# One order of loops, one set of addresses and one pool size in a two-layer hybrid block

## The chip, the core and the metric

The kernel runs on 1 core of one Trainium2 chip. The metric is the device time of one execution in microseconds (us). Five queues of instructions run beside each other: PE (TensorE, matrix products), ACT (ScalarE), DVE (VectorE), POOL (GpSimd) and SP (SyncE, which here issues transfers). PEld is the loading of the stationary operand of a product on PE.

## The reference, cut to what matters

Two layers run one after the other on `x`, 512 rows of 1024 floats. A layer normalises the rows, multiplies them by `w_in` (1024 x 9312), feeds the columns of the product to three mixers (an mLSTM, a gated linear attention and a sparse attention that picks 128 keys for each query), and multiplies what they give by `w_out` (2048 x 1024).

```python
p = split_columns(rmsnorm(x, norm_g) @ w_in)
...
y = jnp.concatenate([y_ml, y_gla, y_dsa], axis=-1) @ w_out
return x + y
```

All is float32. The kernel forms each product with `w_in` and `w_out` from two halves of each operand, `hi` (rounded to a one-pass format) and `lo` (what is left), as hi·hi + hi·lo + lo·hi: three one-pass matmuls (`mm3`) in place of one exact one.

## The kernel before, in words

**Weights.** `w_in` and `w_out` are packed in the order of use into 178 pieces of 128 x 1024 floats, 89 for a layer. A piece is loaded into a place called `raw` by a DMA from SP's queue, ACT makes `hi` of it, DVE makes `lo`, and `raw` is then free. All three come from one ring of 11 places (`W_BUFS`, tag "w"), with at most 3 (`RAWS`) places taken by pieces not yet split. `make_room` issues loads, `prepare` makes one `hi` or one `lo`, `give_back` frees a piece's two places when its last product has been issued, and so lets the next load be issued. A unit (a "wide" product of 512 columns, or a part of `w_out`) has 4 pieces and 96 matmuls.

**Products.** `wide` (output tile `pn`) takes a 128 x 128 slice of `xhi` or `xlo` as the stationary operand and 512 columns of a weight piece as the moving one. `proj_t` (`pt`) takes a slice of weights as the stationary operand and 512 columns (384 for the index queries) of `xhi` or `xlo` as the moving one. `w_out_part` (`pw`) takes a slice of `yhi` or `ylo` as the stationary operand and 512 columns of a weight piece as the moving one. The products inside the mLSTM (`psS` from `ml_q`, `ml_k`; `pom` from `swh`, `swl`, `vah`, `val`) and the index scores (`pss`) are one-pass too; transposes (`psx`, `psq`, `psy`, ...) and the rest are exact float32 products.

**Order in w_out.** Four blocks of 128 rows (`sb` 0 to 3) and two halves of 512 columns give 8 chunks of 12 matmuls, each a sum over two pieces. Chunks go in pairs of blocks: half 0 of blocks 0 and 1, half 1 of blocks 0 and 1, then the same for blocks 2 and 3. A piece is given back when block 3 has used it. `wide` already runs its last two blocks side by side: both blocks use piece 0, then both piece 1, and so on.

**Planner.** The order of all instructions is written out by the Python program as it runs. `Meter` gives every instruction a cost, `Clock` keeps a planned time for each engine, and `Background` emits steps of the mixers (with their transposes and small products) between products, at each `tick`, when their planned due time is not later than PE's planned time. A one-pass product of 512 columns costs max(512, 256)/2210 + 0.002 = 0.2337 us in this plan, a transpose 0.109.

**Addresses.** In each partition the program's tiles lie one pool after another, each rounded up to 32 bytes. In the program of this kernel `xhi` starts at byte 36064 and `xlo` at 52448, both 32 past a multiple of 64. The places for weights start at 75072 and the 4 KB tiles of tag "t4" (`yhi`, `ylo`, `ml_q`, `ml_k`, `ik`, ...) at 120128: both are multiples of 64, and so is every place behind them, as each is 4096 bytes long. `vah` starts 32 past a multiple, `val` on one, the eight `swh` and `swl` tiles 32 past.

Of the kernel before, what the change touches and what calls it, by code (L numbers as in the profile page):

```python
# [10 lines left out]
F32 = mybir.dt.float32  # L11
# [148 lines left out]
def free_size(ap):  # L160
    return math.prod(ap.shape[1:])


class Meter:
# [16 lines left out]
    def cost(self, op, args, kw):  # L181
        out = args[0]
        if op == "dma_start":
            return None
        if self.name == "pe":
            if op == "transpose":
                return 0.109
            n, one_pass = free_size(out), kw["rhs"].dtype == F32R
            if one_pass:
                return max(n, 256) / 2210 + 0.002  # L190
            if out.shape[0] == 64:
                return max(n / 950, 0.08)
            return max(4 * n, 256) / 2400 + 0.004
        n = free_size(args[1]) if op == "max" else free_size(out)
        pointers = sum(hasattr(v, "ap") and free_size(v) == 1 for v in (*args[2:], *kw.values()))
        accum = kw.get("accum_out") is not None
        if self.name == "act":
            switch = self.clock.ln != (args[2] == AF.Ln)
            self.clock.ln = args[2] == AF.Ln
            return 0.155 + n / 1138 + 0.09 * pointers + 0.12 * accum + 1.3 * switch  # L200
        if self.name == "dve":
            return 0.15 + n / 945 + 0.06 * min(pointers, 1) + 0.02 * accum
        if kw.get("op") == OP.pow:
            return 0.45 + 0.15 * n
        return 0.1 + n / (510 if op == "tensor_tensor" else 600) + 0.1 * (op == "tensor_tensor")


class Clock:
# [4 lines left out]
    def __init__(self):  # L213
        self.at = dict(pe=0.0, act=0.0, dve=0.0, pool=0.0, sync=0.0)
        self.now = 0.0
        self.ln = True
        self.written, self.touched = {}, {}
        self.rings = {}

    def begin(self):  # L220
        self.now = self.at["pe"]
# [112 lines left out]
def hybrid_kernel(ctx, tc, a, out, dbg=None):  # L334
# [12 lines left out]
            nc.gpsimd.dma_start(dbg[name], ap)  # L347

    ctx.enter_context(tc.manual_schedule())
    N_T4, N_T2 = 11, 19  # L350
    W_BUFS, RAWS, LOAD = 11, 3, 4.5
    const = ctx.enter_context(tc.tile_pool(name="const", bufs=1))
    par = ctx.enter_context(tc.tile_pool(name="par", bufs=2))
    wp = ctx.enter_context(tc.tile_pool(name="wp", bufs=2))
# [6 lines left out]
    def pp(name):  # L361
        t = psp.tile([128, 512], F32, tag="pp", name=name)
        clock.ring("pp", t, 3)
        return t
# [35 lines left out]
    nc.vector.memset(head, 0.0)  # L400
    for odd, r in enumerate(HALVES):
        nc.vector.memset(head[r, odd:odd + 1], 1.0)
    xhi = const.tile([128, KT, S], F32R, name="xhi")
    xlo = const.tile([128, KT, S], F32R, name="xlo")
    qzs = [const.tile([128, 2, 64 * NB], F32, name=f"qz{i}") for i in range(2)]
    for t in qzs:
        for odd, r in enumerate(HALVES):
            nc.gpsimd.memset(t[r, 1 - odd], 0.0)
    lev = const.tile([128, len(LEVELS), 32], U8, name="lev")


    def rstd_of(ss, n, dim, rs, scale=1.0):
# [75 lines left out]
    def need(p):  # L488
        while p.parts is None:
            if not half_done:  # L490
                clock.at["pe"] = max(clock.at["pe"], to_split[0].loaded)
            prepare()
        return p.parts
# [10 lines left out]
    def give_back():  # L504
        p = held.pop(0)
        wanted.remove(p)
        state["used"] -= 2
        make_room()
# [7 lines left out]
    def mm3(ps, lh, ll, rh, rl, first, last):  # L516
        nc.tensor.matmul(ps, lhsT=lh, rhs=rh, start=first, stop=False)
        nc.tensor.matmul(ps, lhsT=lh, rhs=rl, start=False, stop=False)
        nc.tensor.matmul(ps, lhsT=ll, rhs=rh, start=False, stop=last)
# [148 lines left out]
    for layer in range(DEPTH):  # L668
# [53 lines left out]
        def w_out_part(q, yt, tasks, after=None):  # L722
            pieces = take("out", 512 * q)

            def chunk(sb, half):
                bg.drain(tasks[sb])
                s = slice(128 * sb, 128 * sb + 128)
                c = slice(512 * half, 512 * half + 512)
                ps = pp("pw")
                for k in range(4):  # L730
                    wh, wl = need(pieces[2 * half + k // 2])
                    yhi, ylo = (t[k // 2][:, k % 2, s] for t in yt)
                    mm3(ps, yhi, ylo, wh[k % 2], wl[k % 2], k == 0, k == 3)
                    if k % 2:
                        if sb == NB - 1:
                            give_back()
                        if k == 1:
                            tick()
                nc.vector.tensor_tensor(xr[:, sb, c], ps, xr[:, sb, c], op=OP.add)
                if after == "store":  # L740
                    nc.sync.dma_start(out[0, s, c], xr[:, sb, c])
                elif after == "norm" and half:
                    norms.append(norm_task(layer + 1, sb))
                tick()

            for pr in range(2):
                for half in range(2):
                    for sb in (2 * pr, 2 * pr + 1):
                        chunk(sb, half)

# [64 lines left out]
        def scores(i, iqs, ikh, ikl):  # L817
            n = 128 * (i + 1)
            iw = L["iw"]
            acc = wk.tile([128, n], F32, tag=f"acc{i}", name=f"acc{i}", bufs=1)  # L820

            def add(h, rel):
                sc = iw[:, 8 * i + h:8 * i + h + 1]
                if h == 0:
                    nc.vector.tensor_scalar(acc, rel, sc, None, op0=OP.mult)
                else:
                    nc.vector.scalar_tensor_tensor(acc, rel, sc, acc, op0=OP.mult, op1=OP.add)

            pend = []
            for pair in range(4):  # L830
                pss = [pa("pss") for _ in HALVES]
                qs = [iqs[pair // 2][pair % 2][:, odd, 128 * (i - 1):128 * i] for odd in range(2)]
                for q, ps in zip(qs, pss):
                    nc.tensor.matmul(ps[:, 0:n], lhsT=q, rhs=ikh[:, 0:n], start=True, stop=False)
                for r, q, ps in zip(HALVES, qs, pss):
                    nc.tensor.matmul(ps[:, 0:n], lhsT=q[r], rhs=ikl[r, 0:n], start=False, stop=True)
                for p in pend:
                    add(*p)
                pend = []
                for odd, ps in enumerate(pss):  # L840
                    rel = t2("relu", n)
                    nc.scalar.activation(rel, ps[:, 0:n], AF.Relu, scale=0.125)
                    pend.append((2 * pair + odd, rel))
                yield
            for p in pend:
                add(*p)
            D_(f"score{i}", acc)
            nc.gpsimd.memset(acc[0:64, n - 64:n], NEG_INADM)
            accs[i] = acc
            yield  # L850
# [430 lines left out]
        def ml_unit(h):  # L1281
            got, dst, convs, va, t_va = {}, {}, [], [], []
            states[h] = got
            for which, name in enumerate(("ml_q", "ml_k")):
                def part(b, ps):
                    if which not in dst:
                        if not which:
                            bg.drain(t_gates, *(t_scores if h else ()))
                            products_done(h)
                        dst[which] = [blocks(t4(name, dtype=F32R), 2) for _ in range(2)]  # L1290
                    convs.append(bg.start(conv(dst[which], ps, b, 8 * which + 2 * h + b), "conv"))
                chunks_t(take("in", OFF[name] + 256 * h), part)
            done["ml", h] = [bg.add(ml_values(h, got, hn_m), "mlv")]
            bg.add(ml_products(h, dst[0], dst[1], convs, got, done["ml", h - 1] if h else []), "ml")
            so = blocks(t4("so"), NB)

            def part(sb, ps):
                d = so[:, sb, :]
                nc.scalar.activation(d, ps[:, 0:256], AF.Tanh, scale=0.5)
                nc.gpsimd.tensor_scalar(d, d, 0.5, 0.5, op0=OP.mult, op1=OP.add)  # L1300
                if not va:
                    if h:
                        bg.drain(*done["ml", h - 1])
                    va.extend(wk.tile([128, NB, 258], F32R, tag=n, name=n, bufs=1) for n in ("vah", "val"))
                    for t, v in zip(va, (1.0, 0.0)):
                        nc.gpsimd.memset(t[:, :, 256:258].bitcast(F32), v)
                t_va.append(bg.start(split_task([(ps[:, 256:512], va[0][:, sb, 0:256], va[1][:, sb, 0:256])]), "split"))
            wide(take("wide", OFF["ml_o"] + 256 * h), part)
            got["values"] = (so, va, t_va)
# [42 lines left out]
```

## Time and profile before

| | us |
|---|---|
| median of 3 runs | 1228.73 (1228.69 to 1230.84) |
| the profiled execution | 1227.63 |
| its span, first to last instruction | 1225.9 |
| PE busy | 1198.3 (98% of the span) |
| DVE busy | 835.1 (68%) |
| ACT busy | 600.6 (49%) |

The shares of busy time are means over the span; a matmul's busy time is longer than its share of a dense run, since matmuls overlap, so what a matmul costs is read from the distance between starts. Idle time of an engine is put down to what released it.

### The profile page before, as it was taken

How to read it: one execution, taken by the hardware profiler on the slowest of the kernel's cores; microseconds unless marked ns; L12 is line 12 of the kernel's file. 1: busy time of each engine (PE TensorE's matmuls, PEld its weight loads, DVE VectorE, ACT ScalarE, POOL GpSimd, SP SyncE). 2: the span in 40 equal slices, each digit the busy share in tenths (PEclk: the TensorE clock that was granted, in tenths of full speed). 3: DMA queues.
4: the chain of work that ended last, by engine and by line, in shares of the span. 5: the costliest groups of instructions: out<-in, count | busy, mean ns of one | idle time of the engine just before them, and what ended most of it. 6: DMA issues, size and time to landing. Idle time of an engine off the chain costs nothing. (4 is left out here: it accounts for less than half of the span.)

```text
span 1225.9 us, 16513 instructions
## 1 busy us (share of the span) xinstructions
PE 1198.3 (98%) x6004; PEld 970.6 (79%) x6004; DVE 835.1 (68%) x1650; ACT 600.6 (49%) x1334; POOL 171.0 (14%) x309
## 2 busy tenths in 40 slices
PE   6999899999999999999999999999999999999998
PEld 4877687888888887788879777888788888778887
DVE  5477797876777765355555888879867867544644
ACT  6565446554344354652366654474443443555421
POOL 2001221321000010210010023031210000122000
PEclk8999999999999999999999999999999999999999
DMA  5333122212332234132124222222222223233221
GB/s 195 108 98 104 44 92 72 86 61 55 105 108 69 70 119 129 53 112 86 69 70 128 63 86 79 80 73 86 71 70 86 79 85 104 70 112 112 69 82 73
DMA packets 35152, 107.70 MB, mean 88 GB/s; under 512 B 5028, under 2 KB 8388, under 8 KB 35072
## 3 DMA queue, kind: packets, MB, share of 16 engines
q1 hardware_dynamic: 33136, 104.89, 26.5%
q0 software_dynamic: 1200, 1.36, 0.3%
q8 instruction: 47, 0.77, 0.3%
q10 hardware_dynamic: 736, 0.41, 0.1%
q14 instruction: 33, 0.27, 0.1%
HBM read 104.48 MB, written 3.43 MB: 88 GB/s over the span
## 5 line engine op out<-in xcount | busy, mean ns | idle before, releaser
L178 DVE TENSOR_TENSOR lo<-raw,hi 128x1024 fp32r<-128x1024 f32 x178 | 219.1, 1231 | 140.2 <-ACT hi L178 133.5
L178 PE MATMUL pn<-hi,xhi 128*128 128x512 f32 x768 | 313.4, 408 | 0.4 <-ACT xhi L178 0.4
L178 PE MATMUL pn<-lo,xhi 128*128 128x512 f32 x768 | 305.2, 397 | 4.1 <-DVE lo L178 4.1
L178 PE MATMUL pn<-hi,xlo 128*128 128x512 f32 x768 | 304.1, 396 | 0.0
L178 ACT ACTIVATE hi<-raw 128x1024 fp32r<-128x1024 f32 x178 | 188.7, 1060 | 197.9 <-PE pn L178 96.8
L178 PEld LDWEIGHTS pn<-lo,xhi 128*128 128x128 f32 x768 | 145.1, 189 | 37.7 <-DVE lo L178 7.0
L178 PEld LDWEIGHTS pn<-hi,xlo 128*128 128x128 f32 x768 | 144.6, 188 | 35.8 <-DVE xlo L178 1.3
L178 PEld LDWEIGHTS pn<-hi,xhi 128*128 128x128 f32 x768 | 145.1, 189 | 33.2 <-issue 0.8
L178 PE MATMUL pt<-xhi,hi 128*128 128x512 f32 (+1 forms) x400 | 159.1, 398 | 0.0
L178 PE MATMUL pt<-xhi,lo 128*128 128x512 f32 (+1 forms) x400 | 154.6, 387 | 0.0
L178 PE MATMUL pt<-xlo,hi 128*128 128x512 f32 (+1 forms) x400 | 154.5, 386 | 0.0
L178 PE MATMUL pw<-hi,yhi 128*128 128x512 f32 x256 | 102.1, 399 | 0.8 <-DVE zz L178 0.8
L178 PE MATMUL pw<-hi,ylo 128*128 128x512 f32 x256 | 100.0, 391 | 0.0
L178 PE MATMUL pw<-lo,yhi 128*128 128x512 f32 x256 | 99.8, 390 | 0.0
L178 PEld LDWEIGHTS pt<-xhi,hi 128*128 128x128 f32 x400 | 75.2, 188 | 18.0 <-issue 3.9
L178 PEld LDWEIGHTS pt<-xhi,lo 128*128 128x128 f32 x400 | 75.3, 188 | 15.3
L178 PEld LDWEIGHTS pt<-xlo,hi 128*128 128x128 f32 x400 | 75.5, 189 | 12.7
L178 DVE TENSOR_TENSOR xr<-pw,xr 128x512 f32<-128x512 f32 x64 | 44.2, 690 | 58.7 <-PE pw L178 58.7
L178 DVE SCALAR_TENSOR_TENSOR cacc<-cbuf,pv,cacc 128x512 f32<-128x512 f32 x96 | 73.3, 763 | 2.5 <-ACT el L178 0.2
L178 PEld LDWEIGHTS pw<-hi,yhi 128*128 128x128 f32 x256 | 48.1, 188 | 10.5 <-DVE zz L178 1.2
L178 PEld LDWEIGHTS pw<-hi,ylo 128*128 128x128 f32 x256 | 48.0, 188 | 10.3
L178 PEld LDWEIGHTS pw<-lo,yhi 128*128 128x128 f32 x256 | 48.2, 188 | 9.3
(187 smaller groups left out, 1671.0 us busy)
## 6 DMA issues: line engine op xcount, KB each, us to landing
raw<-w_pack SPq DMA_DIRECT2D x178, 512.0 KB, 3.5
xr<-x SPq DMA_DIRECT2D x4, 512.0 KB, 7.3
negm<-negm SPq DMA_DIRECT2D x8, 256.0 KB, 3.7
bs<-skew SPq DMA_DIRECT2D x8, 256.0 KB, 4.0
out_dram<-xr SPq DMA_DIRECT2D x8, 256.0 KB, 2.0
bs<-skew SPq DMA_DIRECT2D x8, 192.0 KB, 4.5
skew<-flat POOLq DMA_DIRECT2D x1, 1280.0 KB, 16.1
bs<-skew SPq DMA_DIRECT2D x8, 128.0 KB, 4.5
```

The costliest lines, as they stand in the source:

```text
L178: return f(*args, **kw)
```

## The change

The last two blocks of rows in `w_out_part` use each piece one after the other (block 2, block 3, next piece), as `wide` does, and a piece is given back when block 3 has used it; there is a tick after every two k-steps of a block. A 32-byte tile `pad` is put ahead of `xhi`; `lev`, `acc3`, `vah` and `val` are lengthened (by 32 bytes each), so that `xhi`, `xlo`, `vah`, `val` and the `swh`, `swl` tiles start at multiples of 64 (`xhi` at 36096, the places for weights at 75136, t4 at 124288). The ring for weights has 12 places in place of 11, of which at most 2 (before 3) are for pieces not yet split; tag "t4" has 10 in place of 11. The planner adds 0.085 us to the first transpose or exact product after a one-pass product.

```diff
             if op == "transpose":
-                return 0.109
+                switch = self.clock.leave()
+                self.clock.projecting = False
+                return 0.109 + switch
             n, one_pass = free_size(out), kw["rhs"].dtype == F32R
+            switch = 0.0 if one_pass else self.clock.leave()
+            self.clock.projecting = one_pass
             if one_pass:
                 return max(n, 256) / 2210 + 0.002
             if out.shape[0] == 64:
-                return max(n / 950, 0.08)
-            return max(4 * n, 256) / 2400 + 0.004
+                return max(n / 950, 0.08) + switch
+            return max(4 * n, 256) / 2400 + 0.004 + switch
...
+    def leave(self):
+        return 0.085 * self.projecting
...
-    N_T4, N_T2 = 11, 19
-    W_BUFS, RAWS, LOAD = 11, 3, 4.5
+    N_T4, N_T2 = 10, 19
+    W_BUFS, RAWS, LOAD = 12, 2, 4.5
...
+    pad = const.tile([128, 8], F32, name="pad")
+    nc.vector.memset(pad, 0.0)
     xhi = const.tile([128, KT, S], F32R, name="xhi")
...
-    lev = const.tile([128, len(LEVELS), 32], U8, name="lev")
+    lev = const.tile([128, 8, 32], U8, name="lev")[:, 0:len(LEVELS)]
...
-            def chunk(sb, half):
-                bg.drain(tasks[sb])
+            pss = {}
+
+
+            def part(sb, i):
+                half = i // 2
+                if i % 2 == 0:
+                    if not half:
+                        bg.drain(tasks[sb])
+                    pss[sb] = pp("pw")
                 s = slice(128 * sb, 128 * sb + 128)
                 c = slice(512 * half, 512 * half + 512)
-                ps = pp("pw")
-                for k in range(4):
-                    wh, wl = need(pieces[2 * half + k // 2])
+                wh, wl = need(pieces[i])
+                for j in range(2):
+                    k = 2 * (i % 2) + j
                     yhi, ylo = (t[k // 2][:, k % 2, s] for t in yt)
-                    mm3(ps, yhi, ylo, wh[k % 2], wl[k % 2], k == 0, k == 3)
-                    if k % 2:
-                        if sb == NB - 1:
-                            give_back()
-                        if k == 1:
-                            tick()
-                nc.vector.tensor_tensor(xr[:, sb, c], ps, xr[:, sb, c], op=OP.add)
-                if after == "store":
-                    nc.sync.dma_start(out[0, s, c], xr[:, sb, c])
-                elif after == "norm" and half:
-                    norms.append(norm_task(layer + 1, sb))
+                    mm3(pss[sb], yhi, ylo, wh[j], wl[j], k == 0, k == 3)
+                if sb == NB - 1:
+                    give_back()
+                if i % 2:
+                    nc.vector.tensor_tensor(xr[:, sb, c], pss.pop(sb), xr[:, sb, c], op=OP.add)
+                    if after == "store":
+                        nc.sync.dma_start(out[0, s, c], xr[:, sb, c])
+                    elif after == "norm" and half:
+                        norms.append(norm_task(layer + 1, sb))
                 tick()
 
-            for pr in range(2):
-                for half in range(2):
-                    for sb in (2 * pr, 2 * pr + 1):
-                        chunk(sb, half)
+            for half in range(2):
+                for sb in range(2):
+                    for i in (2 * half, 2 * half + 1):
+                        part(sb, i)
+            for i in range(4):
+                for sb in (2, 3):
+                    part(sb, i)
...
-            acc = wk.tile([128, n], F32, tag=f"acc{i}", name=f"acc{i}", bufs=1)
+            acc = wk.tile([128, n + 8 * (i == 3)], F32, tag=f"acc{i}", name=f"acc{i}", bufs=1)[:, 0:n]
...
-                    va.extend(wk.tile([128, NB, 258], F32R, tag=n, name=n, bufs=1) for n in ("vah", "val"))
+                    va.extend(blocks(wk.tile([128, 1040], F32R, tag=n, name=n, bufs=1)[:, 0:NB * 258], NB)
+                              for n in ("vah", "val"))
```

## Rows read from the trace of the kernel before

**Rows 1.** The page: busy time of PE, its tenths and its granted clock in 40 slices.

```profile
PE 1198.3 (98%) x6004; PEld 970.6 (79%) x6004; DVE 835.1 (68%) x1650; ACT 600.6 (49%) x1334; POOL 171.0 (14%) x309
PE   6999899999999999999999999999999999999998
PEclk8999999999999999999999999999999999999999
```

**Rows 2.** Groups of PE's instructions, shapes apart: tiles, shape, count, busy us, mean ns.

```profile
L178 PE MATMUL pn<-hi,xhi 128*128 128x512 f32 x768 | 313.4, 408 | 0.4 <-ACT xhi L178 0.4
...
L178 PE MATMUL pt<-xhi,hi 128*128 128x512 f32 x336 | 137.4, 409 | 0.0
...
L178 PE MATMUL pw<-hi,yhi 128*128 128x512 f32 x256 | 102.1, 399 | 0.8 <-DVE zz L178 0.8
...
L178 PE MATMUL pom<-vah,swh 128*128 128x258 f32 x80 | 23.2, 290 | 0.0
...
L178 PE MATMUL pt<-xhi,hi 128*128 128x384 f32 x64 | 21.7, 339 | 0.0
```

**Rows 3.** Chain of work that ended last, merged: start us, us, what.

```profile
919.38 16.35 PE pw L178 x72
935.74 22.48 PE pt L178 x96
958.22 14.01 PE pn L178 x60
972.22 1.39 PE psS L178 x6
...
1014.54 2.77 PE pw L178 x12
...
1017.76 16.36 PE pw L178 x72
1034.11 16.80 PE pn L178 x72
```

**Rows 4.** PE in order of time: start us, us, instruction; three stretches.

```profile
8.32 1.97 PE L178 MATMUL psx<-ident,xs 128*128 128x128 f32 x8 [8.32 <-ACT xs L178]
...
315.06 0.60 PE L178 MATMUL psy<-ident,so 128*128 128x128 f32 x4
315.42 0.47 PE L178 MATMUL pw<-hi,yhi 128*128 128x512 f32 x1
315.74 0.39 PE L178 MATMUL pw<-lo,yhi 128*128 128x512 f32 x1
...
318.04 0.40 PE L178 MATMUL pw<-hi,ylo 128*128 128x512 f32 x1
...
1205.26 0.60 PE L178 MATMUL psy<-ident,dsa_v 128*128 128x128 f32 x4
```

**Rows 5.** Who waited for whom: us in total, times, longest.

```profile
ACT hi L178 <- PE pn L178: 96.8, 59, 6.6
...
ACT hi L178 <- PE pw L178: 76.8, 25, 10.0
...
PE pn L178 <- DVE lo L178: 4.1, 6, 1.9
```

**Rows 6.** ACT and DVE at the end of a w_out part.

```profile
1034.15 1.06 ACT L178 ACTIVATE hi<-raw 128x1024 fp32r<-128x1024 f32 x1 [0.53 <-PE pw L178]
...
1034.76 2.53 DVE L178 TENSOR_TENSOR lo<-raw,hi 128x1024 fp32r<-128x1024 f32 x2
```

**Rows 7.** DMA issues: size of one, median us from issue to landing.

```profile
raw<-w_pack SPq DMA_DIRECT2D x178, 512.0 KB, 3.5
```

**Rows 8.** The last matmul and the last addition, in order of time.

```profile
1221.83 0.39 PE L178 MATMUL pw<-hi,ylo 128*128 128x512 f32 x1
1222.25 0.69 DVE L178 TENSOR_TENSOR xr<-pw,xr 128x512 f32<-128x512 f32 x1 [2.03 <-PE pw L178]
```

**Rows 9.** A stretch of the second layer: PE, PEld, DVE, ACT, POOL busy, clock.

```profile
675.00:920.00 245.00, 243.54 (x1328) 194.03 (x1327) 199.83 (x358) 129.65 (x273) 50.14 (x91) 1.00 0.24 75
```

More of the change, by code (lines that the diff above doesn't have):

```diff
@@ L216, in __init__ @@
         self.ln = True
+        self.projecting = False
         self.written, self.touched = {}, {}
         self.rings = {}
+    def leave(self):
+        return 0.085 * self.projecting
     def begin(self):
```

## The prediction

> **What bounds the kernel now.** I read the page first: PE is busy 1198.3 of 1225.9 us in 6004 matmuls, its tenths are 9 in nearly every slice, and the granted clock is at its upper level (2.4 GHz) from the second slice on [rows 1]. So little is to be won by filling gaps, and the question is what one matmul costs. The groups of PE's instructions give the counts: each of the three forms of `pn` comes 768 times (2304 matmuls), each of `pt` with 512 columns 336 times (1008), with 384 columns 64 times (192), each of `pw` 256 times (768), each of `pom` 80 times (240) [rows 2]. Their mean durations overlap and say nothing of the rate, so I took the rate from the chain of waits, where dense runs stand as one piece [rows 3]: `pw` 16.35/72 = 227.1 and 16.36/72 = 227.2 ns; `pn` 14.01/60 = 233.5 and 16.80/72 = 233.3 ns; `pt` 22.48/96 = 234.2 ns. The three do the same work, one pass over 512 columns with a new stationary operand each time. `pw` and `pn` even take the same kind of moving operand, a weight piece; they differ in the stationary one, `ylo`/`yhi` against `xlo`/`xhi`. By the addresses, all that `pw` reads starts at a multiple of 64 bytes, while `xhi` and `xlo`, stationary in `pn` and moving in `pt`, start 32 past one. That is the reading on which the forecast stands. It is the one difference that I see that fits both, but it is read off a correlation: a difference by region of memory would look the same.
>
> **The change part by part.** The sum is made against the profiled execution's 1227.6 us (span 1225.9 and 1.7 around it); the median of the runs shown, 1228.7, lies 1.1 above, and I add that at the end.
>
> Addresses. Where every 512-column `pn` and `pt` falls to the rate of the `pw` runs of 72, 2304 x 6.2 ns = 14.3 and 1008 x 7.0 ns = 7.1, together 21.4 us: the upper end. But `pw` itself is slower in short runs. The two pieces of 12 ahead of the 72, of which one is shown, take 2.77/12 = 230.8 ns each [rows 3], and behind a transpose, where the first distance is 315.74 - 315.42 = 0.32 us, the next ten take (318.04 - 315.74)/10 = 230 ns [rows 4], where `pn` stays near 233. At 230.8 ns throughout, the gain is 2304 x 2.5 + 1008 x 3.4 = 9.2 us: the lower end, if addresses are the reason. A loss I exclude: only `x` moves against the 64-byte grid among the operands of `pn` and `pt`, to the places in the grid that `w` and `y` already have. A whole part of `w_out`, 12 + 12 + 72 matmuls, has (2.77 + 2.77 + 16.36)/96 = 228.1 ns; at that rate 2304 x 5.2 + 1008 x 6.1 = 18.1 us. `pn` and `pt` are broken up more often than `pw`: of 134 returns from transposes and exact products to one-pass work (between the first and the last group shown [rows 4]), 3312 matmuls at `pw`'s density of 2 in 96 would hold 69, and about 45 come on top; each costs some 10 x 2.9 = 29 ns, so 1.3 us. I take 18.1 - 1.3 = 16.8 us. The 192 `pt` of 384 columns and the 240 `pom` have no aligned run to compare with: between 0 and 432 x 7 ns = 3.0 us, and I take 0, because the six aligned `psS` run at 1.39/6 = 231.7 ns, hardly better than `pn` [rows 3].
>
> Twelve places, two of them for unsplit pieces. ACT waited 96.8 us on `pn` and 76.8 us on `pw` before a `hi` [rows 5]: splits are held up by places, not by ACT. At the end of a part of `w_out` the last `hi` starts at 1034.15, as the next unit starts (1034.11), and the last two `lo` end at 1037.29 [rows 3, 6], 1.0 us ahead of the fourth piece's first need (18 matmuls on, 1038.3). In six places it came too late: PE waited 4.1 us for `lo` [rows 5]. With 11 places and three unsplit pieces beside the 8 places of a unit in use, no split can begin ahead; with 12 and two, the next unit's first piece is split there, and the four splits become three in the same stretch. A split is 1.06 + 1.27 us [rows 6], so the spare time grows by about that. Most of the 4.1 us goes; I take 3.5. Bounds: 4.1 gained, or, if with two in flight a load is late by what its landing (3.5 us [rows 7]) exceeds 12 matmuls (2.7 us) at each of the 8 parts, 6.4 lost. What is late next is a transpose's ACT or DVE work, which this leaves alone.
>
> Side by side. The matmuls stay 96 a part, the ticks 16. Piece 0 is given back 6 matmuls earlier (after 60 in place of 66), piece 2 after 84 in place of 90, which gives the third and fourth splits of the next unit 6 x 0.23 = 1.4 us more; it is in the 3.5. PSUM gets tighter: block 3's second half takes the bank of block 2's first half 12 matmuls (2.7 us) after that sum is finished, where before 24 passed. The addition ends 1222.94 - 1221.83 = 1.1 us after the last matmul's start [rows 8], so 1.6 us are spare, and even one `lo` (1.27) ahead of it on DVE fits. Cost 0; if DVE were 3 us late there, 8 x 1.4 = 11 us. The last stores still follow the last matmul, so the tail stays.
>
> Ten t4 tiles. In the order of before never more than 10 are in use at once, and the one taken next has been free for over 100 instructions even with 10: cost 0. If a conv had to wait once for a group of `psS` (1.4 us) in each of 8 heads, 11 us; PE's order of work covers that.
>
> The planner's 0.085 us. It moves background steps by fractions of a tick. No instruction is added but one memset. Waits of PE come and go by this; from the six rows' worth of 4.1 us I bound it at 4 either way, and charge 1.0, since a faster PE meets ACT and DVE a little earlier. DVE, the busiest after PE, has 199.8 of 245.0 us in its densest stretch [rows 9], so it does not become the bound.
>
> Sum: 1227.6 - 16.8 - 3.5 + 1.0 = 1208.3, and 1.1 for the level: 1209.4 us.
>
> **The rivals.**
>
> (a) The address is not the reason, and `pn` and `pt` stay at 233 and 234 ns. For it: `psS`, aligned on both sides, runs at 231.7 ns, and 72 in a row of `pw` differ from `pn` by memory region too. Against: the three rates are the same in every long run. Time: 1228.7 - 3.5 + 1.0 = 1226.2. The Trainium skill, in "TensorE: Matmul & The Clock Gate", Back-to-back issue gap, gives N/2.4 + 2.5 ns for a warm matmul (an estimate of 215.8 for 512 columns) with no term for an address, and "SBUF — State Buffer", Specifications (TRN2), speaks of lines of 16 bytes, at which a start 32 past a multiple of 64 still lies; by these the first term of my sum is nothing and 1226 is right. The trace does not agree with that page's figure for any of the three (227 at best), so I give it less than the correlation.
>
> (b) Only one role counts, the stationary or the moving operand. If stationary alone: 16.8 x 12.0/18.1 = 11.1 us for `pn`, so 1228.7 - 11.1 - 3.5 + 1.0 = 1215.1; if moving alone, 1220.5. Against it: both roles show the excess today.
>
> (c) Slower: the plan's clock. It still prices 512 columns at 233.7 ns while PE would run near 228.5, and it now adds 0.085 us at each of some 134 changes. PE then reaches each planned transpose ahead of its ACT or DVE work and waits there. Over the run the plan would be late by 3312 x 5.2 ns + 134 x 0.085 = 28.6 us; given back in full at the transposes, that turns 1209.4 - 1.0 into 1237. It decides from 20.3/134 = 0.15 us a change on. Against: `pw` is already 6 ns faster than its price, and the transposes that follow it (315.06) stand without idle time [rows 4].
>
> **How the numbers follow.** Forecast 0.68, (a) 0.13, (b) 0.12, (c) 0.07. The forecast's own range is 1201 to 1219: 1228.7 - 21.4 - 4.1 - 2 for one end, 1228.7 - 9.2 - 3.5 + 3 for the other. To leave no more than 2 in 10 out, the range goes to 1200 to 1226.5, which takes in (b) and about half of (a). A measurement of this kernel tells from no change what is over 0.2% (2.5 us) away: faster holds the forecast, (b) and half of (a), 0.86; the same, the other half of (a), 0.07; slower, (c), 0.07.
>
> **What would show it.** Dense runs of `pn` and `pt` at 227 to 230 ns for the addresses; unchanged at 233 to 234 is (a), one of the two changed is (b). PE's wait for `lo` below 1 us in total for the 12 places. No idle time ahead of the third piece of block 3 in `w_out`. For (c), idle time ahead of transposes, put down to ACT or DVE, summing to over 20 us. The forecast is wrong if PE's distances fall and the span does not, or if the span falls with the distances as they are.

## The result, and the profile after

The changed kernel takes 1209.99 us (median of 4, 1209.58 to 1210.67) against 1229.47 (median of 4, 1228.69 to 1230.84): a ratio of 0.9841 with a 95% interval of 0.9824 to 0.9858, some 19.5 us less. The forecast was 1209.4. The number is right and the reason given for it is wrong: most of the gain is in waits and clock, and the matmuls run at almost the rate that they had.

The page of the kernel after: PE is busier in share, and the granted clock is in the top tenth from the first slice on.

```profile
PE 1190.5 (99%) x6004; PEld 970.7 (80%) x6004; DVE 832.7 (69%) x1651; ACT 600.4 (50%) x1334; POOL 169.6 (14%) x309
PE   6999999999999999999999999999999999999998
PEclk9999999999999999999999999999999999999999
```

The chain of waits after (start us, us, what), the pieces that answer to [rows 3]:

```profile
905.02 16.35 PE pw L178 x72
921.37 22.39 PE pt L178 x96
943.76 16.80 PE pn L178 x72
...
1019.43 16.74 PE pn L178 x72
```

`pn` takes 16.80/72 = 233.3 ns as before, elsewhere 232.5; `pt` 233.2 in place of 234.2. With `xhi` on a multiple of 64, both should have been at 227 to 230 if the forecast's first term held. What did go away stands in the view of who waited for whom, after (us in total, times, longest), which answers to [rows 5]; the last four lines are all of PE's waits:

```profile
ACT hi L178 <- PE pn L178: 90.3, 55, 3.9
...
ACT hi L178 <- PE pw L178: 57.6, 12, 8.2
```

```profile
PE psx L178 <- ACT xs L178: 11.9, 2, 8.4
PE psga L178 <- DVE qz L178: 1.1, 1, 1.1
PE psst L178 <- ACT kdn L178: 0.7, 1, 0.7
PE pn L178 <- DVE lo L178: 0.6, 1, 0.6
```

The same view of the kernel before has two more waits of this size that the forecast did not price, beside the 4.1 us for `lo`:

```profile
PE psq L178 <- ACT qn L178: 4.1, 2, 2.2
...
PE psga L178 <- DVE qz L178: 2.7, 1, 2.7
```

Here `qz` is an operand that DVE makes for the gated linear attention (PE's product with it is `psga`), and `qn` the queries and keys of the sparse attention, which ACT scales by `rq` and PE then transposes (`psq`).

I summed the distances between starts on PE, by what stands at either end, for both profiles (spans 1225.9 and 1208.5, 17.4 us apart; the profiled execution of the kernel before, 1227.63 us, is faster than its four timed runs, so the medians lie further apart). These sums are my own, and no view shows them as they stand: idle time behind another engine 15.5 to 6.0 us, the price of stretches at the lower clock 4.5 to 1.7, changes between one-pass and other work 43.7 to 41.0 (134 returns to 127), distances between 512-column one-pass matmuls 958.3 to 955.0, all else 1.0 more. Of the fall at the lower clock some 1.7 us lie in the first 26 us, where the lower level lasts 6.83 us before and 3.41 after. That part is not the change's: with `x` in phase (below) the order of instructions is the same as after, and it is 6.83 us again.

The wait for `qz` costs twice in the kernel before. The stretch behind it in the kernel before, by busy time of PE, PEld, DVE, ACT and POOL and the granted clock (the figure ahead of the last two):

```profile
140.00:145.00 5.00, 2.54 (x11) 1.70 (x10) 4.92 (x8) 2.35 (x6) 3.43 (x5) 1.00 0.00 0
145.00:149.00 4.00, 3.76 (x23) 3.15 (x24) 1.41 (x4) 0.00 (x0) 0.25 (x1) 0.57 0.02 4
```

and the same work after:

```profile
130.00:136.00 6.00, 4.52 (x19) 3.12 (x17) 5.83 (x9) 0.00 (x0) 0.00 (x0) 1.00 0.40 131
136.00:140.00 4.00, 3.79 (x30) 3.19 (x31) 2.28 (x4) 2.83 (x6) 2.41 (x6) 1.00 0.02 4
```

Before, PE worked 2.54 of 5 us, and then stood at the lower level (1.2 GHz) for most of the next 4 (3.41 us); after, with a wait of 1.1 us, the clock stays. The second cost does not follow each such wait: a kernel below has a wait of 2.8 us without it.

The wait for `qn` is a matter of queues. SP's queue and POOL before (the second `dsa_qk` unit, which makes such `qn`, starts at 480.46):

```profile
474.37 9.50 SPq L178 DMA_DIRECT2D raw<-w_pack  x4
483.97 3.71 SPq L178 DMA_DIRECT2D bs<-skew  x8
```

```profile
487.75 4.81 POOL L178 TENSOR_TENSOR bs<-bs,sel 128x512 f32<-128x512 f32 x6 [27.77 <-DMA bs<-skew]
492.65 0.19 POOL L178 TENSOR_SCALAR rq<-rq 128x4 f32<-128x4 f32 x1
```

```profile
493.97 1.28 ACT L178 ACTIVATE qn<-qn,rq 128x128 f32<-128x128 f32 x4 [5.94 <-POOL rq L178]
```

and after (that unit starts at 472.81):

```profile
466.73 6.37 SPq L178 DMA_DIRECT2D raw<-w_pack  x3
473.20 2.75 SPq L178 DMA_DIRECT2D bs<-skew  x6
```

```profile
477.05 4.81 POOL L178 TENSOR_TENSOR bs<-bs,sel 128x512 f32<-128x512 f32 x6 [24.22 <-DMA bs<-skew]
481.95 0.19 POOL L178 TENSOR_SCALAR rq<-rq 128x4 f32<-128x4 f32 x1
```

The bias rows `bs` are loaded on SP's queue behind loads of weights that stand there until a place is free. Before, four of these were ahead; after, three. POOL starts on `bs` 4.2 us into the unit in place of 7.3, and `rq`, which is behind `bs` on POOL and which `qn` and PE's transposes wait for, comes some 3 us earlier. The wait of 2 us in each layer is gone.

### The profile page after: what moved, and what is told of

It is laid out like the page before. It is cut to its first block, busy times and chain, and to the rows that moved or that the text cites. A ratio compares the mean times of both kernels' runs of the same rounds, so it can differ in the third digit from the quotient of the medians.

```text
span 1208.5 us, 16501 instructions
## 1 busy us (share of the span) xinstructions
PE 1190.5 (99%) x6004; PEld 970.7 (80%) x6004; DVE 832.7 (69%) x1651; ACT 600.4 (50%) x1334; POOL 169.6 (14%) x309
## 4 chain that ended last, share of the span: by engine, by line
PE 88%; DVE 1%; issue 0%; ACT 0%; ACTq 0%
PE pn L178 42%; PE pt L178 17%; PE pw L178 14%; PE psS L178 3%; PE pom L178 2%; PE psga L178 1%; PE pod L178 1%; PE psl L178 1%; PE pog L178 1%; PE psy L178 1%; PE pst L178 1%; PE pss L178 1%; PE psq L178 1%; PE psx L178 0%; PE psst L178 0%; PE psd L178 0%
```

## The experiments

All times are medians against runs of the kernel before on the same chip, or single runs where that is said. The kernel before has medians of 1229.47, 1229.05, 1228.04 and 1228.37 us on the occasions used, so a difference between two kernels measured on different occasions is good to some 1.4 us.

**Which part carries the gain.** Four kernels leave one part out, two have one part alone on the kernel before, and one has three unsplit pieces among the 12 places.

Addresses left out:

```diff
-    pad = const.tile([128, 8], F32, name="pad")
...
-    lev = const.tile([128, 8, 32], U8, name="lev")[:, 0:len(LEVELS)]
+    lev = const.tile([128, len(LEVELS), 32], U8, name="lev")
...
```

> The changed kernel with the addresses of before (no pad, no longer lev, acc3, vah, val; xhi and xlo 32 past a multiple of 64); PE's order of instructions is the same. If the addresses carry the gain, as forecast: 1210 + 16.8 = 1227 us, dense pn at 233.4 ns against 227 to 230 with them. If the gain is stalls and clock, as the profile after suggests (its dense pn run of 72 still takes 16.80 us): 1210 + 0 to 3 us, from the 0.7 ns of a mean pn and 1.2 ns of a mean pt by which the two profiles differ.

1212.54 us, ratio 0.9868 (0.9851 to 0.9885), the second theory. Its dense runs of `pt` and `pn` have the rates of before:

```profile
922.50 22.48 PE pt L178 x96
944.98 16.81 PE pn L178 x72
```

The addresses as changed are worth some 2.6 us, not 16.8.

Places left out:

```diff
-    N_T4, N_T2 = 10, 19
-    W_BUFS, RAWS, LOAD = 12, 2, 4.5
+    N_T4, N_T2 = 11, 19
+    W_BUFS, RAWS, LOAD = 11, 3, 4.5
```

> The changed kernel with 11 places for weights, 3 of them for unsplit pieces, and 11 t4 tiles, as before; all else changed. If the places for weights carry the gain of the stalls: PE waits for lo again, 3 to 4 us in total, and the clock may fall in the stretch at 130 to 150 us, 1215 to 1219 us. If the planner's price or the order in w_out does it: 1210 to 1212 us.

1228.59 us, ratio 0.9998 (0.9987 to 1.0009): without the places nothing is left of the gain, more than either theory allowed. The waits for `qn` are longer than before (7.4 us against 4.1). Who waited for whom on PE in it:

```profile
PE psq L178 <- ACT qn L178: 7.4, 4, 3.0
PE pn L178 <- DVE lo L178: 4.6, 4, 2.2
```

and the granted clock behind one of the waits for `qn`, in two stretches (columns as above):

```profile
484.00:488.20 4.20, 2.02 (x10) 1.35 (x8) 2.78 (x13) 0.00 (x0) 4.03 (x8) 1.00 0.03 6
488.40:495.10 6.70, 6.17 (x22) 5.16 (x23) 0.67 (x4) 5.72 (x16) 0.04 (x1) 0.50 0.00 0
```

Planner's price left out:

```diff
-        return 0.085 * self.projecting
+        return 0.0
```

> The changed kernel with the planner's 0.085 us taken back to 0; all else changed. If the price only shuffles steps: 1210 us within 2. If it is what took PE's waits before psq (2 times 2 us) and qz (2.7 us, and 1.7 us of half clock behind it) away: these come back and it takes 1215 to 1218 us.

1217.78 us, ratio 0.9917 (0.9894 to 0.9939), the second theory for `qz`; but `qn` stayed away:

```profile
PE psga L178 <- DVE qz L178: 5.9, 3, 2.8
```

The longest of these waits ends at 143.35, and the clock stays behind it (columns as above):

```profile
139.00:143.40 4.40, 1.60 (x9) 1.01 (x8) 4.29 (x8) 2.20 (x5) 2.85 (x4) 1.00 0.00 0
143.40:150.00 6.60, 6.60 (x44) 5.61 (x45) 3.67 (x8) 1.98 (x3) 1.13 (x2) 1.00 0.01 4
```

This profile is of the fastest of the four runs (1215.39 us, mean granted clock 0.999), and its span is 4.8 us above the changed kernel's, as much as its waits for `qz` are longer (5.9 against 1.1). The other three runs take 1217.71, 1217.86 and 1220.17 us with mean granted clocks of 0.997, 0.997 and 0.994. That the rest of the 7.8 us between the medians is the clock fits these, but no trace shows it.

Order of `w_out` left out:

```diff
...
-            for i in range(4):
-                for sb in (2, 3):
-                    part(sb, i)
+            for pr in range(2):
+                for half in range(2):
+                    for sb in (2 * pr, 2 * pr + 1):
+                        chunk(sb, half)
...
```

> The changed kernel with the order of w_out_part of before; all else changed. If the order in w_out has a part in the gain beside the 12 places: PE's wait for lo goes from 0.6 to 2 or 3 us and the w_out parts lose as much, 1212 to 1215 us. If the 12 places carry it alone: 1210 us within 1.5.

1209.56 us, ratio 0.9847 (0.983 to 0.9864), and the wait for `lo` is 0.6 us as with the new order. The order in `w_out` is worth nothing that can be measured beside the 12 places.

Places alone, on the kernel before:

```diff
-    N_T4, N_T2 = 11, 19
-    W_BUFS, RAWS, LOAD = 11, 3, 4.5
+    N_T4, N_T2 = 10, 19
+    W_BUFS, RAWS, LOAD = 12, 2, 4.5
```

> The kernel before with 12 places for weights, 2 of them for unsplit pieces, and 10 t4 tiles; addresses, w_out's order and the planner's price as before. If the places carry the gain of the stalls by themselves, as the changed kernel without them (1228.6) suggests: 1229 - 15 = 1214 us or less. If they need the planner's price or the new order beside them (without the price 1217.8 was measured): 1217 to 1225 us.

1222.13 us, ratio 0.9946 (0.9929 to 0.9964), the second theory. Its waits on PE, and the stretch behind the longest of them:

```profile
PE psga L178 <- DVE qz L178: 6.3, 4, 2.9
...
PE pn L178 <- DVE lo L178: 0.5, 1, 0.5
```

```profile
140.00:144.00 4.00, 1.54 (x7) 0.92 (x5) 3.92 (x7) 2.20 (x5) 2.43 (x4) 0.99 0.00 0
144.00:150.70 6.70, 6.22 (x28) 5.08 (x29) 2.34 (x5) 0.07 (x1) 0.49 (x2) 0.50 0.01 2
```

`lo` and `qn` are gone, `qz` has grown from 2.7 to 6.3 us, and PE stands at the lower level for 6.7 us behind it.

Price alone, on the kernel before:

```diff
...
+            switch = 0.0 if one_pass else self.clock.leave()
+            self.clock.projecting = one_pass
...
+    def leave(self):
+        return 0.085 * self.projecting
```

> The kernel before with the planner's 0.085 us alone. If the price needs the 12 places to be worth anything, as the changed kernel without them suggests: 1228 to 1231 us. If it is worth its 7.8 us by itself: 1221 us.

1227.47 us, ratio 0.9991 (0.9982 to 1.0001): half a us below the first theory's stretch, and worth nothing by itself that can be measured. Its profile has no wait for `qz`, but those that are the places' part:

```profile
PE psq L178 <- ACT qn L178: 5.8, 3, 3.0
PE pn L178 <- DVE lo L178: 3.8, 5, 1.8
```

Three unsplit pieces among 12 places:

```diff
-    W_BUFS, RAWS, LOAD = 12, 2, 4.5
+    W_BUFS, RAWS, LOAD = 12, 3, 4.5
```

> The changed kernel with 3 places for unsplit pieces again, of 12. If it is the first split made ahead that counts, which 8 + 3 places do not leave room for: PE's wait for lo is back above 2 us, 1214 to 1220 us. If the twelfth place counts by itself: 1210 us within 2.

1213.39 us, ratio 0.9876 (0.9861 to 0.9891): a little below the first theory's stretch, with its sign; `lo` is waited for in three places again:

```profile
PE pn L178 <- DVE lo L178: 2.4, 3, 2.0
```

The longest, 2.0 us, stands in the unit right behind the first layer's last part of `w_out`, where the prediction's working has the first split come too late. So the limit of two is worth some 3 us of the places' part, and the twelfth place with the ten t4 tiles the rest.

**Why `pw` is faster than `pn` and `pt`.** The changed addresses did not settle it. `w` and `y` do not only start at multiples of 64, they also start at the same place modulo 4096, since every tile between them has 4096 bytes; `x` does not. The next kernel moves `x` to that place, by creating it ahead of `sel2`, `sel3` and the small tiles:

```diff
+    sel0 = const.tile([128, 128], BF16, name="sel0")
+    sel1 = const.tile([128, 256], BF16, name="sel1")
+    xhi = const.tile([128, KT, S], F32R, name="xhi")
+    xlo = const.tile([128, KT, S], F32R, name="xlo")
     mhalf = const.tile([128, 8], F32, name="mhalf")
...
-    xhi = const.tile([128, KT, S], F32R, name="xhi")
-    xlo = const.tile([128, KT, S], F32R, name="xlo")
```

> The changed kernel with xhi and xlo moved from 36096 to 34176, so that they start at the same place modulo 4096 as the weights, which the y tiles of pw do too; nothing else moves, PE's order is the same. If pw is faster because stationary and moving operand lie in phase: pn and pt at 227 to 228 ns, 3312 x about 5.5 ns = 18 us less, 1192 us. If it is the region of memory, or something that is not an address: pn and pt as they are, 1210 us within 2.

1194.92 us, ratio 0.9726 (0.9709 to 0.9743). Its chain of waits, start us, us, what:

```profile
894.25 16.35 PE pw L178 x72
910.60 21.76 PE pt L178 x96
932.36 16.32 PE pn L178 x72
```

`pn` and `pt` are at 226.7 ns. This kernel beats both: 15.1 us below the changed one, 34 below the one before.

The same with `x` 256 bytes (modulo 512) and the t4 tiles, `y` among them, 128 bytes past the weights, by a tile of 128 bytes ahead of t4 and another order of small tiles:

```diff
+    ypad = wk.tile([128, 32], F32, tag="ypad", name="ypad", bufs=1)
...
```

> The changed kernel with xhi and xlo 256 bytes, modulo 512, past the start of the weight places (before 416, changed 384, 0 in the kernel with x in phase), and the t4 tiles, y among them, 128 past; acc3's 32 bytes are left out. A look at the rates. If what counts is the offset between stationary and moving operand modulo 512: pw now leaves 227 ns, and equals what pn does at an offset of 128 in the kernel that is sent with this one; pn between 225 and 240 ns. If it is the region of memory after all: pw stays at 227.

One run, 1199.71 us:

```profile
895.88 16.80 PE pw L178 x72
912.68 21.80 PE pt L178 x96
934.48 16.33 PE pn L178 x72
```

The roles are exchanged: `pw` is now slow, at 233.3 ns, and `pn` and `pt` are fast, at 226.8 and 227.1. So it is neither the region of memory nor the product. Nor is it the place of one operand by itself: in the changed kernel `x` starts on a multiple of 256 (36096), and `pn` is slow.

`x` 128 and t4 64 bytes past:

```diff
+    ypad = wk.tile([128, 16], F32, tag="ypad", name="ypad", bufs=1)
...
+    sels = [const.tile([128, 128 * (i + 1)], BF16, name=f"sel{i}") for i in range(1, NB)]
+    xhi = const.tile([128, KT, S], F32R, name="xhi")
+    xlo = const.tile([128, KT, S], F32R, name="xlo")
+    sel0 = const.tile([128, 128], BF16, name="sel0")
...
```

> The same with xhi and xlo 128 and the t4 tiles 64 past, modulo 512. If the offset counts: pn here equals pw at 128 in the kernel that is sent with this one; pw at 64 lies between its 227 at 0 and that. All of these are multiples of 64, so if 64-byte alignment counted by itself all four rates would be alike.

One run, 1212.72 us:

```profile
905.24 16.80 PE pw L178 x72
922.04 22.39 PE pt L178 x96
944.44 16.80 PE pn L178 x72
```

All are slow, with every operand on a multiple of 64. The expectation had `pw` at 64 between fast and slow; it is slow. `pn` at 128 has the 16.80 that `pw` has at 128 in the kernel before it.

`x` 192 and t4 32 bytes past:

```diff
+    ypad = wk.tile([128, 8], F32, tag="ypad", name="ypad", bufs=1)
...
+    xhi = const.tile([128, KT, S], F32R, name="xhi")
+    xlo = const.tile([128, KT, S], F32R, name="xlo")
+    mhalf = const.tile([128, 8], F32, name="mhalf")
...
+    pad = const.tile([128, 24], F32, name="pad")
...
```

> The changed kernel with xhi and xlo 192 and the t4 tiles 32 bytes past the weight places, modulo 256. A look at the rates of two offsets that no kernel had. If only an offset of 0 modulo 256 is fast: pn and pw both 232 to 234 ns. If the half below or above 128 is, one of them at 227.

One run, 1207.58 us. Neither expectation quite: `pw` at 32 is slow, `pn` at 192 lies between.

```profile
902.10 16.79 PE pw L178 x72
918.89 22.40 PE pt L178 x96
941.29 16.50 PE pn L178 x72
```

Phase alone, on the kernel before (`x` created ahead of the small tiles, with a pad of 64 bytes that moves the weights and `y` along; nothing else):

```diff
...
+    xhi = const.tile([128, KT, S], F32R, name="xhi")
+    xlo = const.tile([128, KT, S], F32R, name="xlo")
+    mhalf = const.tile([128, 8], F32, name="mhalf")
...
+    head = const.tile([128, 2], F32, name="head")
+    const.tile([128, 16], F32, name="pad")
```

> The kernel before with nothing changed but the addresses: xhi and xlo start at the same place modulo 256 as the weights (35968 and 75136, by a pad of 64 bytes and another order of small tiles); PE's order is that of before. If the phase modulo 256 is what sets the rate: pn and pt at 227 to 228 ns, 3312 x 5.4 ns = 18 us less, 1210 us. If the rate only mattered beside the other changes: above 1215 us.

1214.13 us, ratio 0.9886 (0.9869 to 0.9902), between the two expectations.

```profile
907.66 16.37 PE pw L178 x72
924.04 21.76 PE pt L178 x96
...
1020.63 16.32 PE pn L178 x72
```

The rates are as expected, in the unchanged order of instructions. The 4 us short of the expectation are outside the 512-column matmuls: these take 941.4 us of start-to-start distances against 958.3, 16.9 less, while the price of the lower clock rose from 4.5 to 7.7 us (beside the start, it stands behind a wait of 2.1 us for `lo` and, in both layers, behind the wait for `qn`).

## Why the prediction was right, and where it was wrong

**The addresses (16.8 us): wrong, 2.6 us measured.** The correlation was read rightly as far as it went: an address sets the rate, and some 15 us could be had by one (1210.0 to 1194.9 with `x` in phase). But of two properties that `w` and `y` share and `x` lacks, I took the one that the change names, a start on a multiple of 64. The property that counts is the distance between the two operands modulo 256, which in the changed kernel is 128. The 2.6 us are of the size that goes with the table below: 1.0 ns less for each `pt` (96 to 128) and 0.2 to 1.0 for each `pn` (160 to 128). In a side term, the 1.3 us taken off for broken runs, a count is wrong: the trace before has 24 returns to `pw` in its 8 parts, 3 in 96 matmuls and not 2, and 104 to `pn` and `pt`, so none came on top. The prediction's own test was the dense runs: "The forecast is wrong if ... the span falls with the distances as they are." That is what came.

**Rival (a): nearly right on what the change does to the rate, wrong on why, and on the time.** It had `pn` and `pt` unchanged and 1226.2 us, since it took over the small terms for places and price. The address is the reason all the same: the same product of 512 columns takes 226.7 and 233.3 ns in two placements. The Trainium skill, "TensorE: Matmul & The Clock Gate", Back-to-back issue gap, gives the gap by the count of columns without a term for an address: N/2.4 + 2.5 ns for an isolated warm matmul, the only figure that the prediction names, and about 131 ns at 512 columns for a stream of weight loads and matmuls. The runs agree with neither figure.

**Rival (b): no.** With the right offset both roles gain, 6.6 ns for `pn` and 7.5 for `pt` against [rows 3].

**The places (3.5 us): the mechanism held in part, the term was mis-sized.** The wait for `lo` fell from 4.1 to 0.6 us, as worked out, and the first split made ahead is a part of it. But only two of the six waits, 1.6 us, stand in the unit right behind a part of `w_out`, where the working puts them (from 626.42 on); the longest, 1.85 us at 130.06, stands behind units of `pt`. With all else changed the places are worth 18.6 us (1228.6 to 1210.0), and alone 6. I left out what a shorter row of loads does on SP's queue, where `bs` stands behind it (4.1 us of waits for `qn`), and the clock behind a long wait.

**Side by side (0): right**, and so was the spare time of the addition: PE never waits for it in the profile after. **Ten t4 tiles (0)** were not tried by themselves; PE's waits after name none of their writers.

**The price (+1.0): wrong in sign beside the places.** Worth nothing alone, it is worth 7.8 us with them: waits for `qz` are 2.7 us before, 6.3 with the places alone, 5.9 with all but the price, 1.1 with both. PE's order in the traces shows how. The step with the longest wait, the third group of `psga` in the first layer, stands behind 462 matmuls of `pn`, `pt` and `pw` before, with the places alone and with all but the price, and behind 474 in every kernel of these with the price, the price alone included: the price moves it back by 12 matmuls, some 2.8 us. The places leave the first nine groups where they were, and PE comes to the second and third sooner, since of the 1.85 us for `lo` ahead of them some 0.5 is left. Why the same price gives nothing without the places is open in part: there the waits for `qn` are longer (5.8 us against 4.1).

**Rival (c): no.** No wait ahead of `psy`, `psq` or `pst` is left that reaches 0.1 us in total.

So two errors cancelled: some 14 us too much for the addresses, and some 14 us too little for what places and price do to waits and clock. That the total fits is luck.

## What to carry to other kernels

Ahead of any padding, compare the dense runs of products whose operands lie differently, and write down every property in which their addresses differ; here the order in which a few small tiles are created decides over some 15 us. A forecast whose total fits is not confirmed until each of its terms has been found again in a row of the profile after. And where a pool of buffers changes, list what else is issued on the queue of its loads, since what stands behind a load that waits for a place waits with it.

## What the runs showed of the hardware

One-pass matmuls of 512 columns, each with a new stationary operand, in long runs, by the offset of the stationary operand's start from the moving one's, modulo 256:

| offset | ns a matmul | product and kernel |
|---|---|---|
| 0 | 226.7 to 227.4 | `pw` where `y` was not moved against the weights; `pn`, `pt` with `x` in phase and with `x` at 256 |
| 32 | 233.2 | `pw`, t4 at 32 |
| 64 | 233.3 | `pw`, t4 at 64; `pt`, x at 192 |
| 96 | 234.2 | `pt` before and with the addresses left out |
| 128 | 232.5 to 233.3 | `pn`, `pt` after and with `x` at 128; `pw`, t4 at 128 |
| 160 | 233.3 to 233.5 | `pn` before and with the addresses left out |
| 192 | 229.2 | `pn`, x at 192 |

An offset of 256 modulo 512 is as fast as 0. Why 192 lies between, and what in the reading of the two operands makes the difference, is open.

In the stretches shown, the granted clock fell to the lower level behind three waits (PE busy 2.54 of 5.00, 1.54 of 4.00 and 2.02 of 4.20 us), and not behind two others (4.52 of 6.00 and 1.60 of 4.40). What sets the last case apart from the first three is open.
